# Shorter taps in a long depthwise convolution, and two weight units of a projection moved from one exact pass to three split passes

## The chip, the cores and the metric

The kernel runs on one core of a Trainium2 chip. The metric is device time in microseconds (us) of one execution. TensorE (PE in the profile) multiplies matrices, VectorE (DVE) and ScalarE (ACT) do elementwise work, GpSimd (POOL) a little of it, and SyncE (SP) issues the transfers from memory. Each engine works through its own queue in a fixed order; an instruction that waits holds up all that stand behind it in its queue.

## What is computed

Two transformer-like blocks on 256 tokens of 1024 channels, all in float32. The first block normalises the input, multiplies it by `w_in`, and sends the parts to a conformer branch and a state-space branch; their outputs are gated, added and multiplied by `w_o`, and a feed-forward part follows. The second block has two attentions and a mixture of 32 experts. The change lies in the first block:

```python
def causal_dwconv(x, w, b):          # x (B,T,C), w (K,C), b (C)
    k = w.shape[0]
    y = lax.conv_general_dilated(
        x, w[:, None, :].astype(x.dtype), window_strides=(1,),
        padding=[(k - 1, 0)], dimension_numbers=("NWC", "WIO", "NWC"),
        feature_group_count=x.shape[-1])
    return y + b.astype(x.dtype)

def conformer_branch(u_glu, dw_w, dw_b, ln_g, ln_b, w_out):
    a, g = jnp.split(u_glu, 2, axis=-1)
    v = a * jax.nn.sigmoid(g)
    v = causal_dwconv(v, dw_w, dw_b)                  # 31 taps, 1024 channels
    v = jax.nn.silu(layer_norm(v, ln_g, ln_b))
    return v @ w_out

def ssd_branch(...):
    ...
    return yn @ w_out                                 # w_ssm_out, 2048 x 1024

# in the block
mix = (sigmoid(gate_a) * y_a + sigmoid(gate_b) * y_b) @ w_o
```

Output token t of the long convolution is the bias plus the sum over s = 0 to 30 of weight 30 - s times input token t - s; for t - s below 0 there is nothing to add.

## The kernel before

Weights lie in memory as a stream of units of 128 x 2048 float32 (1 MB), read in turn into a ring of five buffers (`stream`, L213). A unit is multiplied in one of two ways (`passes`, L273). In **mode 4** the float32 unit goes straight to TensorE, which takes four times the array's time for it; the profile records each such matmul as two. In **mode 3** the unit is split in halves into a rounded part and a rest, `whl` (`split`, L260): ScalarE writes the rounded part (L261), VectorE the rest (L262), and TensorE then makes three quick matmuls for each one (`order`, L294: high by high, low by high, high by low). Mode 3 is the default; the table `MODES` (L1631) lists the units in mode 4. There are four `whl` buffers (`HL`, L31).

The work of the first block, in the order of the program: normalise; the gated input of the convolution (`glu`, four pairs of units, L597), written by VectorE into `vpad` behind 30 zero columns (L601, zeros at L592); the state-space branch in four groups (L686 to L778); the gates `ga` and `gb` (L793). Then `split_act` (L804) splits the state-space output `ynT` into `ynT_h` and `ynT_l`, and its product with `w_ssm_out` follows in eight units `ws0` to `ws7` of 128 output channels, two per call of `ssm_out` (L806); each call ends in one VectorE instruction on `gate_gb` (L809). `ssm_out(0)` stands ahead of the convolution's taps in the program, `ssm_out(1)` to `(3)` behind them (`WSJ`, L1630).

The convolution is VectorE's alone. `cacc` collects, for each of eight blocks of 128 channels, 31 taps (`tap`, L671): one TENSOR_SCALAR (L674) and 30 SCALAR_TENSOR_TENSOR (L676), each over 256 tokens; two blocks are worked in turn (L813). 8 times 31 are 248 instructions. When all are done, `pair_sums` (L818) adds the blocks in three steps `pair_cs`, TensorE sums over partitions (`cs`, L831), `cacc` is centred (L834), squared by ScalarE into the space of `vpad` (L836), summed again (`cq`, L842), and normalised into `cT`, which the units `wc` multiply (L864) after `ws7`.

The order on each engine is not written by hand. A scheduler takes the program, in which earlier lines come first among the instructions that are ready, plays it through with its own idea of durations, and fixes each engine's queue. So taps of early lines fill VectorE between the urgent instructions of the state-space branch, and every change of a size or of an instruction can move much of the queue.

```python
        for j in range(WSJ):
            ssm_out(j)
        for j in range(0, 8, 2):
            for k in range(CK):
                for i in (j, j + 1):
                    tap(i, k)
...
        for j in range(WSJ, 4):
            ssm_out(j)
```

Of the kernel before, what the change touches and what calls it, by code (L numbers as in the profile page):

```python
# [11 lines left out]
F32 = mybir.dt.float32  # L12
# [5 lines left out]
ALU = mybir.AluOpType  # L18
# [3 lines left out]
P = 128  # L22
T = 256
# [10 lines left out]
CK = 31  # L34
# [156 lines left out]
def block_kernel(ctx, tc, I, out, modes):  # L191
    nc = tc.nc
    V, S, G, PE = nc.vector, nc.scalar, nc.gpsimd, nc.tensor
# [19 lines left out]
    def stream(name):  # L213
        if name in ready:
            return ready[name][0], name
        off, kt, n = OFFSET[name]
        w = ring.tile([P, UNIT], F32, tag="w", name=f"w_{name}")
        src = I["stream"][off:off + P * kt * n].rearrange("(p m) -> p m", p=P)
        nc.sync.dma_start(w[:, :kt * n], src)
        return w[:, :kt * n].rearrange("p (k n) -> p k n", k=kt), name  # L220
# [12 lines left out]
    def par(name, i=0, n=1):  # L233
        second, o = PPO[name]
        return (pp2 if second else pp)[:, o + i:o + i + n]
# [33 lines left out]
    def act(pool, kt, name, tags=("ah", "al"), f=None):  # L269

        return Act(f, *(pool.tile([P, kt, T], F32R, tag=t, name=f"{name}_{t}") for t in tags))
# [40 lines left out]
    def gemm_chan(names, x, pool=mm, between={}):  # L312


        c, banks, put, last = 0, [], None, None
        for name in names:
            w, _ = stream(name)
            ps_ = passes(w, name)
            for i in range(w.shape[2] // P):
                if c % 2 == 0:  # L320
                    banks.append(bank(pool, f"ps_{name}_{i}").rearrange("p (c t) -> p c t", c=2))
                o = banks[-1][:, c % 2, :]
                if c in between:
                    with after(last):
                        put = between[c]()
                c += 1
                m = order(ps_, i * P, P)
                for j, (k, part, wp) in enumerate(m):
                    with after(put):
                        last = PE.matmul(o, wp, getattr(x, part)[:, k, :],  # L330
                                         start=(j == 0), stop=(j == len(m) - 1)).ins
        return banks
# [206 lines left out]
    with ExitStack() as e1:  # L539
        b1 = e1.enter_context(tc.tile_pool(name="b1", bufs=1, reuse_waits="tile"))  # L540
        hT = act(b1, 8, "hT")
        vpad = b1.tile([P, 8, T + CK - 1], F32, tag="vpad", name="vpad")
        cacc = b1.tile([P, 8, T], F32, tag="cacc", name="cacc")
        ynT = Act(b1.tile([P, 16, T], F32, tag="ynT", name="ynT"))
        gate = {n: b1.tile([P, 8, T], F32, name=f"gate_{n}") for n in ("ga", "gb")}
# [5 lines left out]
        with tc.tile_pool(name="pre", bufs=1, reuse_waits="tile") as pre:  # L551
# [15 lines left out]
            with tc.issue_after(hT.last), tc.issue_after(hT.act):  # L567
                ident_b = dcon.tile([P, P], BF16, name="ident_b")
                V.tensor_copy(ident_b, ident)
                ones = dcon.tile([P, P], F32, name="ones")  # L570
                V.memset(ones, 1.0)

                upper = dcon.tile([P, P], F32, name="upper")
                G.affine_select(out=upper, in_=ones, pattern=[[1, P]], compare_op=ALU.is_ge, fill=0.0, base=0, channel_multiplier=-1)
                strict = dcon.tile([P, P], F32, name="strict")
                G.affine_select(out=strict, in_=ones, pattern=[[-1, P]], compare_op=ALU.is_gt, fill=0.0, base=0, channel_multiplier=1)

                before_b = const.tile([P, P], BF16, name="before_b")
                V.tensor_tensor(before_b, upper, ident, op=ALU.subtract)

                pick = dcon.tile([P, 32], BF16, name="pick")
                V.tensor_tensor(pick, ident[:, 0:32], ident[:, 32:64], op=ALU.add)
                V.tensor_tensor(pick, pick, ident[:, 64:96], op=ALU.add)
                ones_b = const.tile([P, P], BF16, name="ones_b")
                V.memset(ones_b, 1.0)

                strict_b = dcon.tile([P, P], BF16, name="strict_b")
                V.tensor_scalar(strict_b, strict, NEG, None, op0=ALU.mult)
                slots = const.tile([P, CAP], F32, name="slots")
                G.iota(slots, pattern=[[1, CAP]], base=0, channel_multiplier=0, allow_small_or_imprecise_dtypes=True)  # L590
                iota8 = slots[:, :8]
                V.memset(vpad[:, :, :CK - 1], 0.0)  # L592
                S.activation(silu_c, par("c_2", 0, 8), AF.Silu)
                V.tensor_copy(cpad[:, :, 0], silu_c)


            for j in range(4):  # L597
                pa, pg = gemm_chan([f"glu{j}a0", f"glu{j}g0"], hT)
                sg = sg_pool.tile([P, 2, T], F32, tag="sg", name=f"sg{j}")
                S.activation(sg, pg, AF.Sigmoid)  # L600
                V.tensor_tensor(vpad[:, 2 * j:2 * j + 2, CK - 1:], pa, sg, op=ALU.mult)  # L601
                if j == 1:
                    nc.sync.dma_start(w_dt, I["w_dt"])
                    nc.sync.dma_start(rs, I["rs"].to_broadcast([P, NRS]))
                    nc.sync.dma_start(pp2, I["pp2"])
# [36 lines left out]
            for i in range(2):  # L642
                q = rs[:, RSO[f"lambda_q{i + 1}_2"]:RSO[f"lambda_q{i + 1}_2"] + 64]
                k = rs[:, RSO[f"lambda_k{i + 1}_2"]:RSO[f"lambda_k{i + 1}_2"] + 64]
# [24 lines left out]


        def tap(i, k):  # L671
            o = cacc[:, i, :]
            if k == 0:
                V.tensor_scalar(o, vpad[:, i, 0:T], par("conv_dw_w", i * CK), par("conv_dw_b", i), op0=ALU.mult, op1=ALU.add)  # L674
            else:
                V.scalar_tensor_tensor(o, vpad[:, i, k:k + T], par("conv_dw_w", i * CK + k), o, op0=ALU.mult, op1=ALU.add)  # L676


        def conv4(dst, ps_, c):
# [133 lines left out]
# [4 lines that stand above are left out]
# [12 lines left out]
        b = bank(sm, "cs")  # L829
        for i in range(2):  # L830
            PE.matmul(b[:, :T], ones, pair[:, i, :], start=(i == 0), stop=(i == 1))  # L831
        csq = vpad[:, :, :T]
        for i in range(0, 8, 2):
            V.scalar_tensor_tensor(cacc[:, i:i + 2, :], b[:, None, :T].to_broadcast(both), -1.0 / D, cacc[:, i:i + 2, :],  # L834
                                   op0=ALU.mult, op1=ALU.add)
# [21 lines left out]
        for n, i in ((4, "h"), (5, "l")):  # L857
            w = late.tile([P, 2, UNIT], F32, tag=f"ynT_{i}", name=f"w_ada{n}")
# [10 lines left out]
        for n in range(2):  # L869
            with tc.issue_after(cT.last):  # L870
                end = ada_v(n)
            for t, ps_ in enumerate(gemm_tok(f"wo{n}", mixT, 8, early=2 * n)):
                o = res[:, t, n * 512:(n + 1) * 512]
# [6 lines left out]
    with ExitStack() as e2:  # L880
# [17 lines left out]
        for j in range(11):  # L898
# [11 lines left out]
            for b, ps_ in enumerate(banks):  # L910
                o = b2.tile([P, 2, T], F32, tag=f"cv{b}", name=f"cv{b}_{j}", bufs=2)
                for i in range(2):
                    c = 22 * b + 2 * j + i
                    scale_bias(o[:, i, :], ps_[:, i, :], par("ffn_dw_w", 3 * c + 2), par("ffn_dw_b", c))
                    for s in range(1, 3):
                        V.scalar_tensor_tensor(o[:, i, s:], ps_[:, i, :T - s], par("ffn_dw_w", 3 * c + 2 - s), o[:, i, s:],
                                               op0=ALU.mult, op1=ALU.add)
# [5 lines left out]
        for n in range(2):  # L923
            end = ada_v(2 + n)
            for t, ps_ in enumerate(gemm_tok(f"dn{n}", guT, 22, early=2 * n)):
                o = res[:, t, n * 512:(n + 1) * 512]
# [22 lines left out]
    with ExitStack() as e3:  # L949
# [152 lines left out]
        for i in range(4):  # L1102
            (p1, r1), (p2, r2) = softmax_parts(qdT, kdT, i, "d")
            V.tensor_scalar(r2, r2, lam[:, 3:4], None, op0=ALU.mult)
            for q in range(2):
                V.tensor_scalar(p2[:, halves[q]], p2[:, halves[q]], r2[:, q:q + 1], None, op0=ALU.mult)
                V.scalar_tensor_tensor(p1[:, halves[q]], p1[:, halves[q]], r1[:, q:q + 1], p2[:, halves[q]],
                                       op0=ALU.mult, op1=ALU.add)
# [172 lines left out]
        for u in range(2):  # L1281
            w, nm = stream(f"wu1_{u}")
# [229 lines left out]
    for p in range(NE // 2):  # L1512
        last = p == NE // 2 - 1
        w = [fetched[12 * p + 2 * i:12 * p + 2 * i + 2] for i in range(6)]
# [113 lines left out]


WSJ = 1  # L1630
MODES = {n: 4 for n in ("ws0", "ws1", "ws2", "ws3", "wo1_1", "dn1_5", "qm_1", "glu0a0")}  # L1631


# [12 lines left out]
```

## Time and profile before

| what | before |
|---|---|
| median of three runs | 1231.01 us (1229.98 to 1234.34) |
| profiled execution | 1230.77 us, of which span 1229.1 us |
| PE busy | 1193.9 us (97%) |
| DVE busy | 778.5 us (63%) |
| ACT busy | 501.5 us (41%) |
| read from memory | 350.68 MB, 286 GB/s over the span |
| L676, the taps | 240 instructions, 100.7 us |

The span is the time from the first to the last instruction in the trace. Two records of one engine may overlap, so the time from start to start can be shorter than an instruction's own duration. The busy share of 63% on DVE is a mean over stages: up to about 300 us into the span it is nearly always busy, later far less. In the last 430 us the experts' weights are read at about 420 GB/s, the highest rate of the profile.

### The profile page before, as it was taken

The numbers are of one execution on the slowest core, as the hardware profiler recorded it, in microseconds if no ns is written. First come the engines' busy times: TensorE is split into PE (matmuls) and PEld (weight loads), VectorE is DVE, ScalarE is ACT, GpSimd is POOL, SyncE is SP. The second block draws the span as 40 slices with busy tenths as digits, with TensorE's granted clock in tenths as the row PEclk, the third lists the DMA queues.
The fourth block names the chain that finished last, engine by engine and source line by source line (L and its number), as shares of the span: only waits on it lengthen the run. The fifth ranks groups of instructions, "written<-read, shape, count | busy, mean of one in ns | idle before, by whom it ended". The sixth has DMA issues, their size and how long they took to land. (4 is left out here: it accounts for less than half of the span.)

```text
span 1229.1 us, 19383 instructions
## 1 busy us (share of the span) xinstructions
PE 1193.9 (97%) x7867; PEld 873.9 (71%) x7867; DVE 778.5 (63%) x1524; ACT 501.5 (41%) x831; POOL 27.5 (2%) x39
## 2 busy tenths in 40 slices
PE   7999999999999999999999999999999999999996
PEld 6989998898978999885888889544444444444443
DVE  6999999899877989667786676623322222332222
ACT  6456787743536666534345554411111111111111
POOL 0000100100000000001000000000000000000000
PEclk9999999999999999999999999999999999999999
DMA  9645343325777656764796347899999999999996
GB/s 361 237 144 198 113 171 104 138 103 206 292 269 296 240 194 219 283 211 167 298 383 268 116 144 294 330 412 421 423 419 423 420 424 420 423 420 423 422 420 244
DMA packets 51917, 353.03 MB, mean 287 GB/s; under 512 B 6000, under 2 KB 6640, under 8 KB 10224
## 3 DMA queue, kind: packets, MB, share of 16 engines
q1 hardware_dynamic: 51824, 351.75, 72.8%
q8 instruction: 63, 1.03, 0.3%
q14 instruction: 30, 0.25, 0.1%
HBM read 350.68 MB, written 1.05 MB: 286 GB/s over the span
## 5 line engine op out<-in xcount | busy, mean ns | idle before, releaser
L1534 DVE TENSOR_TENSOR hid<-hid,pu 128x256 f32<-128x256 f32 x32 | 12.0, 418 | 187.6 <-PE pu L1526 187.6
L1526 PE MATMUL pu<-we,xg 128*64 128x512 f32 x512 | 116.2, 593 | 4.6 <-DMA we<-in_experts 4.6
L1583 PE MATMUL pd<-we,hdT 128*64 128x512 f32 x512 | 113.4, 595 | 1.5 <-DVEq L1422 1.5
L1526 PE MATMUL pg<-we,xg 128*64 128x512 f32 x512 | 113.4, 592 | 0.0
L676 DVE SCALAR_TENSOR_TENSOR cacc<-vpad,pp,cacc 128x256 f32<-128x256 f32 x240 | 100.7, 477 | 0.0
L1526 PEld LDWEIGHTS pu<-we,xg 128*64 128x64 f32 x512 | 37.4, 137 | 80.5 <-issue 69.5
L1526 PEld LDWEIGHTS pg<-we,xg 128*64 128x64 f32 x512 | 37.8, 137 | 72.2 <-issue 69.8
L1583 PEld LDWEIGHTS pd<-we,hdT 128*64 128x64 f32 x512 | 35.9, 137 | 67.7 <-issue 64.9
L261 ACT ACTIVATE osb<-ob 128x512 fp32r<-128x512 f32 x31 | 19.5, 630 | 120.5 <-DVE ob L1587 120.5
L1546 ACT ACTIVATE hdT<-ht 128x512 f32<-128x512 f32 x16 | 9.6, 597 | 142.5 <-PE ht L1545 142.5
L1361 DVE TENSOR_SCALAR xg<-xg,s,mod 128x128 f32<-128x128 f32 x64 | 21.9, 404 | 65.9 <-PE xg L1337 63.7
L341 PE MATMUL ps_dn<-whl_dn,guT_gh 128*128 128x512 f32 x168 | 53.8, 398 | 0.0
L330 PE MATMUL ps_xs<-hT_ah,whl_xs 128*128 128x256 f32 x256 | 47.2, 282 | 0.0
L1587 DVE SCALAR_TENSOR_TENSOR ob<-pd,wpl,g 128x512 f32<-128x512 f32 x31 | 23.3, 751 | 37.4 <-PE pd L1583 34.8
L1529 ACT ACTIVATE hid<-pg 128x512 f32<-128x512 f32 x16 | 9.6, 597 | 82.5 <-PE pg L1526 82.4
L341 PE MATMUL ps_z<-whl_z,hT_ah 128*128 128x512 f32 x128 | 41.6, 398 | 0.1
L330 PEld LDWEIGHTS ps_xs<-hT_ah,whl_xs 128*128 128x128 f32 x256 | 39.6, 188 | 0.0
L341 PEld LDWEIGHTS ps_dn<-whl_dn,guT_gh 128*128 128x128 f32 x168 | 31.6, 188 | 7.7 <-issue 0.2
L495 DVE SCALAR_TENSOR_TENSOR sb_ada<-w_ada,silu_c,sb_ada 128x512 f32<-128x512 f32 x49 | 36.6, 747 | 0.6
L262 DVE TENSOR_TENSOR whl_dn<-w_dn,whl_dn 128x1024 fp32r<-128x1024 f32 x21 | 25.7, 1225 | 17.4 <-ACT whl_dn L261 17.3
L262 DVE TENSOR_TENSOR obl<-ob,osb 128x512 fp32r<-128x512 f32 x31 | 21.5, 693 | 21.6 <-ACT osb L261 21.6
L261 ACT ACTIVATE whl_dn<-w_dn 128x1024 fp32r<-128x1024 f32 x21 | 22.2, 1059 | 30.0 <-PE ps_dn L341 25.4
(760 smaller groups left out, 3111.8 us busy)
## 6 DMA issues: line engine op xcount, KB each, us to landing
we<-in_experts SPq DMA_DIRECT2D x189, 1024.0 KB, 19.8
w_ada<-in_stream SPq DMA_DIRECT2D x22, 1024.0 KB, 7.1
w_dn<-in_stream SPq DMA_DIRECT2D x10, 1024.0 KB, 4.8
w_xs<-in_stream SPq DMA_DIRECT2D x8, 1024.0 KB, 4.8
w_z<-in_stream SPq DMA_DIRECT2D x8, 1024.0 KB, 4.8
w_ws<-in_stream SPq DMA_DIRECT2D x8, 1024.0 KB, 4.8
w_bc<-in_stream SPq DMA_DIRECT2D x4, 1024.0 KB, 4.8
w_ga<-in_stream SPq DMA_DIRECT2D x4, 1024.0 KB, 4.8
```

What stands on the lines that cost most here:

```text
L261: a = S.activation(h, f, AF.Copy)
L262: return a.ins, V.tensor_tensor(l, f, h.bitcast(F32), op=ALU.subtract).ins
L330: last = PE.matmul(o, wp, getattr(x, part)[:, k, :], start=(j == 0), stop=(j == len(m) - 1)).ins
L341: PE.matmul(banks[t], getattr(x, p_)[:, u + k, t * P:(t + 1) * P], wp, start=(u == 0 and j == 0), stop=(u + kt == ktot and j == len(m) - 1))
L495: V.scalar_tensor_tensor(a, w[:, q, :], c, a, op0=ALU.mult, op1=ALU.add)
L676: V.scalar_tensor_tensor(o, vpad[:, i, k:k + T], par("conv_dw_w", i * CK + k), o, op0=ALU.mult, op1=ALU.add)
L1361: spreads.append(V.tensor_scalar(xg[:, k, :], src, s2[:, k:k + 1], mod[:, 24 + k:25 + k], op0=ALU.mult, op1=ALU.add).ins)
L1526: m = PE.matmul(pgu[i // 2][64 * e:64 * e + 64, :], xg[:, 4 * (i % 2) + k, 64 * e:64 * e + 64], w[i][e][:, k, :], start=(i % 2 == 0 and k ...
L1529: S.activation(hd, pgu[0], AF.Silu)
L1534: V.tensor_tensor(hd[:, c], hd[:, c], pgu[1][:, c], op=ALU.mult)
L1583: m = PE.matmul(pd[64 * e:64 * e + 64, :], hdT[:, f, 64 * e:64 * e + 64], w[4 + h][e][:, f, :], start=(f == 0), stop=(f == 3))
L1587: V.scalar_tensor_tensor(o[:, c], pd[:, c], wpl, g2[:, h, c], op0=ALU.mult, op1=ALU.mult)
```

## The change

The convolution's input has no zeros in front any more: `vpad` becomes `vg`, 256 columns wide, and the instruction that wrote the zeros is gone. A tap that reaches back s tokens adds input columns 0 to 255 - s to output columns s to 255, so it covers 256 - s columns. The taps run in the opposite order: the one with s = 0 comes first (it sets all columns and adds the bias), the one with s = 30 last. `csq`, the space for the squares, is now `vg` itself. And `ws2` and `ws3` leave the table `MODES`: they are split and multiplied in three passes as `ws4` to `ws7` were.

```diff
-        vpad = b1.tile([P, 8, T + CK - 1], F32, tag="vpad", name="vpad")
+        vg = b1.tile([P, 8, T], F32, tag="vg", name="vg")
...
-                V.memset(vpad[:, :, :CK - 1], 0.0)
...
-                V.tensor_tensor(vpad[:, 2 * j:2 * j + 2, CK - 1:], pa, sg, op=ALU.mult)
+                V.tensor_tensor(vg[:, 2 * j:2 * j + 2, :], pa, sg, op=ALU.mult)
...
         def tap(i, k):
-            o = cacc[:, i, :]
-            if k == 0:
-                V.tensor_scalar(o, vpad[:, i, 0:T], par("conv_dw_w", i * CK), par("conv_dw_b", i), op0=ALU.mult, op1=ALU.add)
+
+            k = CK - 1 - k
+            o, w = cacc[:, i, CK - 1 - k:], par("conv_dw_w", i * CK + k)
+            if k == CK - 1:
+                V.tensor_scalar(o, vg[:, i, :], w, par("conv_dw_b", i), op0=ALU.mult, op1=ALU.add)
             else:
-                V.scalar_tensor_tensor(o, vpad[:, i, k:k + T], par("conv_dw_w", i * CK + k), o, op0=ALU.mult, op1=ALU.add)
+                V.scalar_tensor_tensor(o, vg[:, i, :T - (CK - 1 - k)], w, o, op0=ALU.mult, op1=ALU.add)
...
-        csq = vpad[:, :, :T]
+        csq = vg
...
-MODES = {n: 4 for n in ("ws0", "ws1", "ws2", "ws3", "wo1_1", "dn1_5", "qm_1", "glu0a0")}
+MODES = {n: 4 for n in ("ws0", "ws1", "wo1_1", "dn1_5", "qm_1", "glu0a0")}
```

The scheduler then lays out the queues anew from about the second group of the state-space branch on. Two places matter. The first is VectorE's queue at the end of the taps (L676 before, L677 now), where `gate_gb` is the end of `ws0` and `ws1`, `pair_cs` the sums of all taps, and `whl_ws` the split of a half unit of `ws`. Before:

```order
L676 SCALAR_TENSOR_TENSOR cacc<-vpad,pp,cacc 128x256 x37
L809 SCALAR_TENSOR_TENSOR gate_gb<-gate_gb,ps_ws_0_2899 128x512
L676 SCALAR_TENSOR_TENSOR cacc<-vpad,pp,cacc 128x256 x23
L821 TENSOR_TENSOR pair_cs<-cacc 128x512
L262 TENSOR_TENSOR whl_ws_0_3275<-w_ws_3273,whl_ws_0_3275 128x1024
L823 TENSOR_TENSOR pair_cs<-pair_cs,cacc 128x512
```

With the change:

```order
L677 SCALAR_TENSOR_TENSOR cacc<-vg,pp,cacc 128x232 x2
L810 SCALAR_TENSOR_TENSOR gate_gb<-gate_gb,ps_ws_0_2898 128x512
L677 SCALAR_TENSOR_TENSOR cacc<-vg,pp,cacc 128x231 x2
L677 SCALAR_TENSOR_TENSOR cacc<-vg,pp,cacc 128x230 x2
L677 SCALAR_TENSOR_TENSOR cacc<-vg,pp,cacc 128x229 x2
L677 SCALAR_TENSOR_TENSOR cacc<-vg,pp,cacc 128x228 x2
L677 SCALAR_TENSOR_TENSOR cacc<-vg,pp,cacc 128x227 x2
L677 SCALAR_TENSOR_TENSOR cacc<-vg,pp,cacc 128x226 x2
L822 TENSOR_TENSOR pair_cs<-cacc 128x512
L262 TENSOR_TENSOR whl_ws_0_3236<-w_ws_3234,whl_ws_0_3236 128x1024
L824 TENSOR_TENSOR pair_cs<-pair_cs,cacc 128x512
```

The number of taps behind `gate_gb` falls from 23 to 12. The first split of `ws` stands behind the last tap and the first `pair_cs` in both, but before it belonged to `ws4` and now it belongs to `ws2`.

The second place is TensorE's queue from the first `ws` unit on (`w_ws` is a unit in mode 4, `whl_ws` a split half; `cs` is the sum over partitions that ends the taps). Before:

```order
L330 MATMUL ps_ws_0_2899<-ynT,w_ws_2897 128x256 x16
L330 MATMUL ps_ws_0_2899<-ynT,w_ws_2916 128x256 x16
L330 MATMUL ps_ws_0_3237<-ynT,w_ws_3235 128x256 x16
L330 MATMUL ps_ws_0_3237<-ynT,w_ws_3254 128x256 x16
L831 MATMUL cs<-pair_cs,ones 128x256 x2
L330 MATMUL ps_ws_0_3281<-ynT_h,whl_ws_0_3275 128x256
```

With the change:

```order
L330 MATMUL ps_ws_0_2898<-ynT,w_ws_2896 128x256 x16
L330 MATMUL ps_ws_0_2898<-ynT,w_ws_2915 128x256 x16
L330 MATMUL ps_ws_0_3242<-ynT_h,whl_ws_0_3236 128x256
L330 MATMUL ps_ws_0_3242<-ynT_l,whl_ws_0_3236 128x256
L330 MATMUL ps_ws_0_3242<-ynT_h,whl_ws_0_3236 128x256
```

Before, four units in mode 4 stood ahead of `cs`. Now two do, and right behind them come matmuls of `ws2` that read a split half; `cs` follows after 26 of those.

## Rows read from the trace of the kernel before

**Rows 1.** The page, busy time of TensorE, and its granted clock in 40 slices.

```profile
PE 1193.9 (97%) x7867; PEld 873.9 (71%) x7867; DVE 778.5 (63%) x1524; ACT 501.5 (41%) x831; POOL 27.5 (2%) x39
...
PEclk9999999999999999999999999999999999999999
```

**Rows 2.** Busy time by stretch: PE, PEld, DVE, ACT, POOL, clock, DMA share, GB/s.

```profile
265.00:280.00 15.00, 15.00 (x71) 13.22 (x70) 15.00 (x39) 2.54 (x3) 0.00 (x0) 1.00 0.26 75
280.00:295.00 15.00, 13.96 (x67) 12.01 (x66) 15.00 (x31) 0.00 (x0) 0.00 (x0) 1.00 0.41 146
```

**Rows 3.** Waits of PE, 264 to 420 us: total, times, longest; the longest one.

```profile
PE cs L831 <- DVE pair_cs L823: 1.0, 1, 1.0
```

**Rows 4.** Waits of PE, 20 to 265 us, all of them.

```profile
PE pcs L659 <- DVE a L656: 0.8, 1, 0.8
PE bt L724 <- DVE xd L716: 0.8, 2, 0.6
```

**Rows 5.** Timeline of PE from `ws0` to `wc`: start, length, instruction, [idle before].

```profile
264.74 27.79 PE L330 MATMUL ps_ws<-ynT,w_ws 128*128 128x256 f32 x128
293.57 1.13 PE L831 MATMUL cs<-pair_cs,ones 128*128 128x256 f32 x4 [1.04 <-DVE pair_cs L823]
294.35 0.47 PE L330 MATMUL ps_ws<-ynT_h,whl_ws 128*128 128x256 f32 x1
294.66 0.28 PE L330 MATMUL ps_ws<-ynT_l,whl_ws 128*128 128x256 f32 x1
...
295.13 0.28 PE L330 MATMUL ps_ws<-ynT_l,whl_ws 128*128 128x256 f32 x1
...
318.61 0.28 PE L330 MATMUL ps_wc<-cT_ah,whl_wc 128*128 128x256 f32 x1
```

**Rows 6.** Timeline of DVE at the end of the taps.

```profile
261.19 3.25 DVE L676 SCALAR_TENSOR_TENSOR cacc<-vpad,pp,cacc 128x256 f32<-128x256 f32 x8
...
265.01 14.73 DVE L676 SCALAR_TENSOR_TENSOR cacc<-vpad,pp,cacc 128x256 f32<-128x256 f32 x37
279.66 0.67 DVE L809 SCALAR_TENSOR_TENSOR gate_gb<-gate_gb,ps_ws 128x512 f32<-128x512 f32 x1
280.26 9.19 DVE L676 SCALAR_TENSOR_TENSOR cacc<-vpad,pp,cacc 128x256 f32<-128x256 f32 x23
289.37 0.68 DVE L821 TENSOR_TENSOR pair_cs<-cacc 128x512 f32<-128x512 f32 x1
289.97 1.21 DVE L262 TENSOR_TENSOR whl_ws<-w_ws,whl_ws 128x1024 fp32r<-128x1024 f32 x1
```

**Rows 7.** Groups of one form: busy us, mean ns of one, for other widths.

```profile
L676 DVE SCALAR_TENSOR_TENSOR cacc<-vpad,pp,cacc 128x256 f32<-128x256 f32 x240 | 100.7, 477 | 0.0
L495 DVE SCALAR_TENSOR_TENSOR sb_ada<-w_ada,silu_c,sb_ada 128x512 f32<-128x512 f32 x49 | 36.6, 747 | 0.6
...
L683 DVE SCALAR_TENSOR_TENSOR xsT<-ps_xs,pp,xsT 128x255 f32<-128x255 f32 x16 | 7.3, 479 | 0.9 <-ACT xsT L681 0.8
...
L683 DVE SCALAR_TENSOR_TENSOR xsT<-ps_xs,pp,xsT 128x253 f32<-128x253 f32 x16 | 7.0, 473 | 0.0
```

**Rows 8.** Timeline of PE: its first instructions, and the same transposes later.

```profile
9.04 1.97 PE L365 MATMUL tr_h<-ident,xn 128*128 128x128 f32 x8 [9.04 <-ACT xn L402]
...
20.52 0.47 PE L330 MATMUL ps_glu0g<-hT_ah,whl_glu0g 128*128 128x256 f32 x1
...
370.01 1.09 PE L365 MATMUL tr_h<-ident,xn 128*128 128x128 f32 x8
```

**Rows 9.** Busy time by stretch, columns as in rows 2: the end of the span.

```profile
1222.00:1225.00 3.00, 0.06 (x1) 0.00 (x0) 1.67 (x5) 1.80 (x5) 1.10 (x2) 1.00 0.07 25
1225.00:1229.00 4.00, 0.00 (x0) 0.00 (x0) 0.40 (x1) 0.37 (x1) 0.00 (x0) 0.71 0.66 243
```

**Rows 10.** The experts: one stretch, columns as in rows 2.

```profile
900.00:950.00 50.00, 49.48 (x304) 22.33 (x302) 14.43 (x40) 7.38 (x16) 0.00 (x0) 1.00 1.01 421
```

**Rows 11.** Waits of SP's queue, 600 to 1229 us: one before the experts.

```profile
SPq L534 <- DVE mgT_kd L1180: 14.9, 1, 14.9
```

## The prediction

> **What bounds the kernel now.** I read the page first: TensorE is busy 97% of the span, so its idle time is the thing to look for [rows 1]. That share is a mean over stages, so I went by stretch to where the change lies. From 265 to 295 us VectorE is busy without a pause and ScalarE, in the second half, does nothing; TensorE loses a little [rows 2]. The waits of TensorE say what that little is: one wait of 1.0 us for `pair_cs`, the end of the taps [rows 3]. Before 265 us all its waits together are 1.6 us [rows 4]. So two engines run level here: TensorE works off the units `ws`, VectorE the taps, and they meet at `cs`. The reader is to see in the two timelines [rows 5, 6] how the meeting is arranged. TensorE spends 27.79 us on `ws0` to `ws3` in mode 4, and none of that needs VectorE. In just that time VectorE does its last 60 taps and `pair_cs`. The four units are the cover of the taps.
>
> **Part 1, the taps get shorter.** The cost per column comes from one instruction at two widths: 477 ns at 256 columns, 747 ns at 512, so (747 - 477) / 256 = 1.05 ns a column [rows 7]. A tap reaching back s tokens loses s columns; 1 to 30 sum to 465, times 8 blocks is 3720 columns, times 1.05 ns is 3.9 us off VectorE. Tap starts at odd columns should cost nothing: the short convolution already writes 253 to 255 columns from column 1, 2 or 3 on, at 473 to 479 ns [rows 7]. The zero-fill of 30 columns is gone too; it lies in the first 30 us, where TensorE is fed by transfers and ScalarE, and I count it as nothing (if it were on the path it could give 0.3 us at most, as it is shorter than a tap of 477 ns). `vg` in place of `vpad`, and the squares written into it, are the same instructions.
>
> **Part 2, `ws2` and `ws3` in three passes.** A unit in mode 4 is 32 records; 128 records took 27.79 us [rows 5], so 6.95 us a unit. In mode 3 it is 48 matmuls, and four of them start 0.47 us apart from first to fifth [rows 5], 0.1175 us each, so 5.64 us. TensorE's own work falls by 2 x 1.31 = 2.6 us. VectorE gets four splits more of 1.21 us [rows 6], about 4.8 us, ScalarE four as well, while it is idle [rows 2]. On balance VectorE's work is about level (-3.9, +4.8).
>
> **Part 3, what the new order does with it.** This decides. The queues shown with the change have `ws2` right behind `ws1` on TensorE, and `ws2` needs its split, which stands on VectorE behind the last tap and the first `pair_cs`. TensorE has nothing else in between: it must stand still from the end of `ws1` until the taps are done. The queue behind the waiting matmul holds `cs`, `ws3` to `ws7`, and `wc`, all of the rest.
>
> - `ws1` ends at 264.74 + 64 x 0.217 = 278.6 us [rows 5].
> - The split of `ws2` ends, reckoned one way, by VectorE's work: taps end at 289.37 less 3.9 = 285.5, `pair_cs` takes 0.60, the split 1.21 [rows 6], so 287.3 us.
> - Reckoned another way, by the order: `gate_gb`, which ends `ws0` and `ws1`, ran at 279.66 [rows 6]. Twelve taps stand behind it with the change, 25 to 30 columns short, each (289.37 - 280.26) / 23 = 0.396 us less 0.029, so 4.4 us together. 279.66 + 0.60 + 4.4 + 0.60 + 1.21 = 286.5 us.
> - It can't be much earlier: `gate_gb` waits for `ws1` at 278.6, which gives 285.4 us.
>
> I take 286.9, midway between the two reckonings. TensorE stands idle for 8.3 us, where it stood 1.04 us.
>
> After that VectorE has the next half unit ready 1.2 to 2.4 us after the last (a `pair_cs` lies between the first ones), and TensorE needs 24 x 0.1175 = 2.8 us for one, so it runs without a pause. From the start of `ws4` to `wc` it took 318.61 - 294.35 = 24.26 us [rows 5]; now 96 matmuls more, 11.3 us, and `cs` (294.35 - 293.57 = 0.78 us) lie in the same stretch: 36.3 us. `wc` starts at 286.9 + 36.3 = 323.2 in place of 318.61, **4.6 us later**. This agrees with the parts: 7.3 us more idle time less 2.6 us of work. With the two reckonings and the earliest case the term is 3.1 to 5.0 us; as TensorE might lose less than its 1.6 us of waits ahead of this place [rows 4], I let it reach down to 1.5.
>
> **Part 4, TensorE's clock.** The trace of before has no idle time of this length between matmuls. It has two places that bound the price. Behind the 1.04 us at `cs` the clock stays at 1.00 [rows 2], price 0. At the start, after 9.04 us without work, eight transposes take 1.97 us where the same eight later take 1.09 [rows 8]: half speed, though the clock column reads 9 or more tenths from the first slice on [rows 1]. And at the end of the span the clock falls to 0.71 in the mean of the last 4 us, while TensorE has done 0.06 us in the 7 us up to there [rows 9], so part of the stretch is on the lower of the two levels, 1.2 GHz. The price of the start: from 9.04 to 20.52 us are 11.48 us for 16 transposes and the 32 records of `glu0a`; at the later pace 2 x 1.09 + 32 x 0.217 = 9.1. That is 2.4 us. An idle of 8.3 us is far nearer to 9.04 than to 1.04, so I take 2.0 us, ends 0 and 2.4.
>
> By the column of the clock alone, which shows no fall before the end, there would be no such term. The Trainium skill (TensorE: Matmul & The Clock Gate, Part 1) says otherwise and speaks against this change: half rate is the default of an idle array, and only activity lifts it. By the column the sum is 1235.4, by the rule 1237.4; the halved pace of the first transposes agrees with the rule.
>
> **The sum.** The profiled execution took 1230.77 us, 0.24 below the median of the runs. 1230.77 + 4.6 + 2.0 = **1237.4 us**. A shift at 318 us reaches the end because TensorE does without a pause what follows, and the experts' transfers, which run at their top rate later [rows 10], are not issued early of their own: their main burst waits for a result of the second block's attention, `mgT` [rows 11], and shifts with it.
>
> **Rivals.**
>
> *The clock holds* (0.14). The idle time comes as reckoned and costs nothing beyond. For it: the column of the clock. Against it: rows 8 and 9. Time 1235.4.
>
> *The experts swallow it* (0.08), no slower than before. In the last stage transfers fill the queues (DMA share 1.01) and TensorE is busy 49.48 of 50 us [rows 10]. If the weights arrived by a clock of their own, the delay would only eat into time that TensorE later spends waiting for them, and the end would stay: 1230.8. The point from which this holds: the burst of rows 11 would have to start at the same time in the run as now. Against it: it waits 14.9 us for VectorE's result, which is late by the same 6.6 us.
>
> *The taps don't get cheaper* (0.08). If short taps cost what long ones do, the taps end at 289.37 as before and the split at 291.2. TensorE is idle 12.6 us, `wc` starts 291.2 + 36.3 = 327.5, 8.9 later, and the clock takes its full 2.4: 1242.1. Against it: the two widths of rows 7.
>
> **How the numbers follow.** A measurement of this kernel can tell about 0.5% from no change, 6.2 us here, so from 1237.2 on it is slower. My forecast has 0.62, and with its terms of 1.5 to 5.0 and 0 to 2.4 it runs from about 1232.5 to 1238.2 and a little beyond for what the new order does elsewhere; its middle is just above the bound, so 0.34 of it is slower and 0.28 the same. The clock's rival (0.14) and the experts' (0.08) are the same, the taps' (0.08) slower. What I have not seen (0.08), such as another course of the state-space groups in the new order, I give 0.03, 0.03 and 0.02 to faster, same and slower. Sums: faster 0.03, same 0.53, slower 0.44. The range for 8 in 10 takes in my forecast, the clock's rival and the experts' case (0.84 together), 1230.0 to 1241.0; it leaves out the taps' case and most of the unseen.
>
> **What would show it.** Taps of L677 falling from 477 ns to about 446 at 226 columns. TensorE idle for 7 to 9 us just ahead of the first `whl_ws` matmul, put down to VectorE's `whl_ws`; `wc` 3 to 7 us later than 318.61; the first matmuls behind the gap at about 0.235 us from start to start in place of 0.1175, if the clock falls. No change of the stretch from `wc` to the end. I would be wrong if that gap is under 4 us (the order doesn't cost what I read from it), or if the end doesn't follow `wc`.

## The result, and the profile after

The changed kernel takes 1243.5 us (median of 6 runs, 1241.8 to 1247.5) where the kernel before took 1231.4 beside it: ratio 1.0106, 95% interval 1.0095 to 1.0116. It is slower by 1.1%, nearly twice what was forecast, and outside the range. The profiled execution took 1243.87 us with a span of 1242.1, 13.0 longer than before.

The page of the changed kernel, TensorE's busy time and granted clock, against [rows 1]:

```profile
PE 1195.1 (96%) x7899; PEld 874.4 (70%) x7899; DVE 779.7 (63%) x1527; ACT 503.9 (41%) x833; POOL 26.9 (2%) x39
...
PEclk9999999998999999999999999999999999999998
```

All engines do as much as before, within 3 us; the 13 us are time in which TensorE stands or works slowly. Setting the starts of the same matmuls side by side in the two traces shows where:

| stretch | lost there (us) | forecast |
|---|---|---|
| start to first `bc` matmul (63.03, now 61.65) | -1.4 | 0 |
| `bc` to `ws0` (264.74, now 266.30) | +2.9 | 0 |
| `ws0` to first `wc` (318.61, now 324.14) | +4.0 | +6.6 |
| `wc` to the last `qm` matmul (585.15, now 592.13) | +1.5 | 0 |
| from there to the last `pu` matmul (1207.29, now 1214.61) | +0.3 | 0 |
| last `pu` to the last `pd` matmul (1218.62, now 1231.70) | +5.8 | 0 |

`bc` is the first product of the state-space branch, `qm` one of the second block's attention; `pu` and `pd` are products of the experts, which are worked in 16 pairs, and `pd` of the last pair is TensorE's last large piece of work.

The stretch that I had reckoned with gives less than forecast, and more than half of the loss lies at places that I had put at nothing. Four stretches of the changed kernel (busy PE, PEld, DVE, ACT, POOL, clock, DMA share, GB/s) show the clock behind three of these places:

```profile
89.00:91.00 2.00, 1.51 (x6) 1.21 (x7) 1.74 (x5) 1.95 (x4) 0.00 (x0) 0.87 0.00 0
91.00:93.00 2.00, 2.00 (x6) 1.62 (x5) 1.99 (x8) 1.99 (x3) 0.00 (x0) 0.50 0.04 8
...
280.00:295.00 15.00, 8.96 (x57) 8.34 (x56) 15.00 (x28) 2.31 (x4) 0.00 (x0) 0.77 0.46 158
...
1223.00:1227.00 4.00, 3.66 (x10) 1.36 (x12) 0.00 (x0) 0.00 (x0) 0.00 (x0) 0.50 0.09 32
```

The third, 280 to 295 us, stands against the second row of [rows 2]: 8.96 us of work where there were 13.96, at 0.77 of the clock where it was 1.00. A clock of 0.50 is the lower level, 1.2 GHz, through the whole stretch.

**Place one, near 89 us.** TensorE's timeline, the `z` matmuls of the first state-space group:

```profile
86.31 0.61 PE L786 MATMUL pdec<-a__111,upper 128*128 128x32 f32 x4
89.49 0.50 PE L341 MATMUL ps_z<-whl_z,hT_ah 128*128 128x512 f32 x1 [2.57 <-ACT zs L704]
```

It waits for `zs`, an activation. ScalarE's timeline there, changed kernel:

```profile
82.19 1.01 ACT L682 ACTIVATE xsT<-ps_xs,pp 128x256 f32<-128x256 f32 x2
86.51 0.56 ACT L682 ACTIVATE bcT<-ps_bc,pp 128x256 f32<-128x256 f32 x1 [3.31 <-DVE bcT L684]
86.98 0.56 ACT L682 ACTIVATE xsT<-ps_xs,pp 128x256 f32<-128x256 f32 x1
87.55 1.28 ACT L704 ACT_TABLE_LOAD   x1
88.84 0.60 ACT L704 ACTIVATE zs<-ps_z 128x512 f32<-128x512 f32 x1
```

and of the kernel before:

```profile
83.40 1.01 ACT L681 ACTIVATE xsT<-ps_xs,pp 128x256 f32<-128x256 f32 x2
84.43 1.28 ACT L703 ACT_TABLE_LOAD   x1
87.58 0.60 ACT L703 ACTIVATE zs<-ps_z 128x512 f32<-128x512 f32 x1 [1.87 <-PE ps_z L341]
88.84 0.57 ACT L681 ACTIVATE bcT<-ps_bc,pp 128x256 f32<-128x256 f32 x1 [0.66 <-DVE bcT L683]
```

Before, the table was loaded and `zs` ran the moment `ps_z` was there. Now `bcT` and `xsT` stand ahead of it, ScalarE waits 3.31 us for VectorE's `bcT`, and only then loads the table. Nothing in this code was edited: the scheduler, with the taps changed, chose another order.

**Place two, `ws2`.** TensorE and VectorE of the changed kernel, against [rows 5] and [rows 6]:

```profile
279.92 0.47 PE L330 MATMUL ps_ws<-ynT_h,whl_ws 128*128 128x256 f32 x1
...
281.87 0.27 PE L330 MATMUL ps_ws<-ynT_l,whl_ws 128*128 128x256 f32 x1
288.19 2.29 PE L330 MATMUL ps_ws<-ynT_h,whl_ws 128*128 128x256 f32 x9 [6.04 <-DVE whl_ws L262]
...
290.53 1.78 PE L832 MATMUL cs<-pair_cs,ones 128*128 128x256 f32 x4
291.96 0.47 PE L330 MATMUL ps_ws<-ynT_h,whl_ws 128*128 128x256 f32 x1
```

```profile
281.30 0.69 DVE L810 SCALAR_TENSOR_TENSOR gate_gb<-gate_gb,ps_ws 128x512 f32<-128x512 f32 x1
281.90 4.50 DVE L677 SCALAR_TENSOR_TENSOR cacc<-vg,pp,cacc 128x231 f32<-128x231 f32 x12
286.30 0.69 DVE L822 TENSOR_TENSOR pair_cs<-cacc 128x512 f32<-128x512 f32 x1
286.90 1.23 DVE L262 TENSOR_TENSOR whl_ws<-w_ws,whl_ws 128x1024 fp32r<-128x1024 f32 x1
```

The wait is the one forecast, for the split behind the last tap. But it stands inside `ws2`: 16 matmuls (high by high and low by high, from 279.92 on) need only ScalarE's rounded half and run ahead of it; the last 8, high by low, need VectorE's rest. From the end of `ws1` to the split, 279.92 to 288.19, it is 8.27 us; 2.2 of them were filled.

**Place three, the last `pd` group.** The changed kernel, then the kernel before:

```profile
1217.53 0.38 PE L1563 MATMUL cm<-ident,ow 128*128 128x128 f32 x2
1223.34 8.95 PE L1584 MATMUL pd<-we,hdT 128*64 128x512 f32 x32 [5.43 <-DMA we<-in_experts]
```

```profile
1210.21 0.38 PE L1562 MATMUL cm<-ident,ow 128*128 128x128 f32 x2
1212.12 7.09 PE L1583 MATMUL pd<-we,hdT 128*64 128x512 f32 x32 [1.53 <-DVEq L1422]
```

A wait of 5.43 us where 1.53 stood, and 8.95 us for the group where it took 7.09: 3.9 and 1.9 us, the 5.8 of the table. The profile names the weights in one and the branch in the other (L1422, now L1423: in `past_capacity`, the one branch in the kernel, which jumps over code that this input does not need). The labels contradict each other, so this place needed experiments.

### The profile page after: what moved, and what is told of

Read it like the earlier page. It is cut to its first block, busy times and chain, and to the rows that moved or that the text cites. A ratio compares the mean times of both kernels' runs of the same rounds, so it can differ in the third digit from the quotient of the medians.

```text
span 1242.1 us, 19456 instructions
## 1 busy us (share of the span) xinstructions
PE 1195.1 (96%) x7899; PEld 874.4 (70%) x7899; DVE 779.7 (63%) x1527; ACT 503.9 (41%) x833; POOL 26.9 (2%) x39
## 5 line engine op out<-in xcount | busy, mean ns | idle before, releaser
L677 DVE SCALAR_TENSOR_TENSOR cacc<-vg,pp,cacc 128x255 f32<-128x255 f32 (+14 forms) x240 | 97.4, 463 | 0.1
L330 PE MATMUL ps_ws<-ynT_h,whl_ws 128*128 128x256 f32 x192 | 35.7, 289 | 6.0 <-DVE whl_ws L262 6.0
```

The lines of the kernel that those rows point to most:

```text
L330: last = PE.matmul(o, wp, getattr(x, part)[:, k, :], start=(j == 0), stop=(j == len(m) - 1)).ins
L677: V.scalar_tensor_tensor(o, vg[:, i, :T - (CK - 1 - k)], w, o, op0=ALU.mult, op1=ALU.add)
```

## Experiments

**e1 and e2: the two halves apart.** e1 is the changed kernel with the old table, e2 the kernel before with the new one.

```diff
-MODES = {n: 4 for n in ("ws0", "ws1", "wo1_1", "dn1_5", "qm_1", "glu0a0")}
+MODES = {n: 4 for n in ("ws0", "ws1", "ws2", "ws3", "wo1_1", "dn1_5", "qm_1", "glu0a0")}
```

> The shortened taps alone; all four units of the state-space output product run in four passes as in the kernel before. Theory: the 12 us are four separate losses, and two of them (6.0 us of idle TensorE ahead of the last 8 matmuls of ws2, and the 5.4 us ahead of the last pd group at the end, which comes from the length of TensorE's own program) go with the passes, while the 2.6 us wait for the zs activation near 86 us goes with the taps, since ScalarE's order there is that of the changed kernel. Then: a wait of about 2.6 us for zs, none at ws2, cs not waiting for pair_cs, and about 1.5 us at the last pd as before; 1232 us (1230 to 1234). Rival A, all of the loss follows from the ws2 wait and taps only help: 1228 us or less (3.9 us of taps less the clock). Rival B, the late pd group is a matter of late weights whatever the program: 5 us more at the end, 1237 to 1238 us.

> The padded full-length taps of the kernel before; only ws2 and ws3 in three passes. Theory: no wait for zs; TensorE runs ws0, ws1 and 16 matmuls of ws2 until about 280.5 us and then stands until the split behind the last tap and the first pair sum ends near 291.2 us, 10 to 11 us; minus 1.0 of the old wait and 2.6 of saved passes, plus about 3 us of half clock: the first wc matmul near 328 us (10 later than before), and 5.4 us at the last pd as in the changed kernel, since TensorE's program has its length: 1246 us (1243 to 1250). Rival A (the ws2 wait is all that the passes cost): 1241 us. Rival B (late weights at the end whatever the program): either.

e1: 1234.52 us, ratio 1.0026 (1.0015 to 1.0038). e2: 1246.79 us, 1.0131 (1.0117 to 1.0146). The longest waits of TensorE, 20 to 420 us, in e1:

```profile
PE ps_z L341 <- ACT zs L704: 2.6, 1, 2.6
PE pcs L658 <- DVE a L655: 1.0, 1, 1.0
PE cs L832 <- DVE pair_cs L824: 0.8, 1, 0.8
```

and in e2:

```profile
PE ps_ws L330 <- DVE whl_ws L262: 10.6, 1, 10.6
```

Each wait follows its half: `zs` the taps, `ws2` and the late `pd` (1.53 us in e1, 5.51 in e2) the passes. Rival A falls in both: the taps alone are slower and not faster, and e2 lies 5.8 us above its 1241. In e1 `cs` still waited 0.8 us, which I had not expected, and the clock fell once more, near 780 us; it came out 2.5 us above my number and just above its range. The halves don't add up (3.7 and 15.9 make 19.6, the whole lost 12.1). Most of that lies at `ws2`, where the changed taps cut the wait from 10.6 to 6.0 us: from `ws0` to `wc` e1 loses 0.4 us, e2 10.2 and the changed kernel 4.0, so 6.6 of the 7.5 us.

**e3 and e4: a longer program for TensorE.** Each kernel with 64 idle matmuls in the expert stage:

```diff
-                m = PE.transpose(b[:, t * P:(t + 1) * P], owf[:, t, :], ident).ins
+                m = PE.transpose(b[:, t * P:(t + 1) * P], owf[:, t, :], ident).ins; [PE.matmul(b[:, 511:512], ident, ident[:, :1], start=True, stop=True) for _ in range(2)]
```

> The kernel before with 64 one-column matmuls added to the expert stage, four in each of the 16 pairs, behind the cm transposes, where TensorE waits for weights from time to time; nothing reads what they write. TensorE's program before the last branch is then as many matmuls longer as that of the changed kernel (64). Theory (the late pd group comes from where the branch's target falls in TensorE's program): the wait ahead of the last pd group grows from 1.5 to about 5.4 us, part of the group runs at half clock, and the time is 1237 us (1235 to 1239). Rival B (late weights): the wait stays near 1.5 us, time 1231 to 1233 us.

> The changed kernel with the same 64 one-column matmuls in the expert stage. Theory: the branch's target moves on by another 64 matmuls with their weight loads; the wait ahead of the last pd group falls from 5.4 to about 1.5 us, with no half clock there, and the time is 1238 us (1236 to 1240). Rival B (late weights, since the stage began 7 us later): 5 us stay, 1243 to 1245 us.

e3: 1235.61 us, 1.0034 (1.0021 to 1.0047), the wait 1.52 us. e4: 1247.74 us, 1.0128 (1.0112 to 1.0145), the wait 4.47 us. Both kept the wait that they had, as rival B has it, and the theory as I had put it falls. (Both take some 4 us more than without the pad, and more than rival B had. The added matmuls are busy 16.1 us in each trace, the waits of `pu` for weights, 4.6 and 5.3 us without the pad, are gone, and near 780 us both have a stretch at half clock.) But the counts showed that this was no test of it. The queue that fetches TensorE's instructions, changed kernel and e4:

```profile
q8 instruction: 63, 1.03, 0.3%
```

```profile
q8 instruction: 64, 1.05, 0.3%
```

One fetch of 16 KB more, and 128 matmuls with their 128 weight loads more in the trace: I had added 256 instructions, just one such page, so that everything behind kept its place in its page. The changed kernel has 32 matmuls and 32 loads more than the one before, 64 instructions.

**e6 and e7: the same with other counts.** The same line with `ident[:1, :1]` in 1 x 1 matmuls, three for each pair of experts in e6 (changed kernel, 48) and one in e7 (kernel before, 16).

> The changed kernel with 48 matmuls of 1 x 1 in the expert stage, three in each pair. In e3 and e4 each added matmul showed as two matmuls and two weight loads in the trace, 256 instructions in all, and one instruction fetch of 16 KB more (64 for 63): a whole page, which left the branch's target where it was in its page. 48 make 192 instructions; with the 64 that the changed kernel has more than the one before that is a whole page again. Theory (the target's place in its page decides): the wait ahead of the last pd group 1.5 us, no half clock there; 1238 us (1236 to 1240). Rival (late weights): about 5 us as in e4, 1243 to 1248 us.

> The kernel before with 16 matmuls of 1 x 1 in the expert stage, one in each pair: 64 instructions, as many as the changed kernel has more. Theory (the branch target's place in its page): the wait ahead of the last pd group grows from 1.5 to about 5 us, 3 to 7 us of half clock follow; 1236 us (1234 to 1239). Rival (late weights): 1.5 us, 1231 to 1232 us.

e6: 1238.6 us, 1.0063 (1.0049 to 1.0077). e7: 1236.63 us, 1.0047 (1.0033 to 1.0061). TensorE's timeline of e6, then of e7:

```profile
1219.97 7.09 PE L1584 MATMUL pd<-we,hdT 128*64 128x512 f32 x32 [1.52 <-DVEq L1423]
```

```profile
1218.24 9.78 PE L1583 MATMUL pd<-we,hdT 128*64 128x512 f32 x32 [5.84 <-PEq L1422]
```

Both turned over. The kernel before, with 16 matmuls whose result nothing reads, gets the late `pd` group; the changed kernel, with 48, loses it. Late weights are excluded: e6 has the same transfers and does not wait. Over all kernels the wait goes by the number of TensorE instructions ahead of the branch, counted from the kernel before and less whole pages of 256:

| more instructions | kernels | wait at the last `pd` (us) |
|---|---|---|
| 0 | before, e1, e3, e5, e6, e11 | 1.5 |
| 32 | e8 | 1.5 |
| 64 | changed, e2, e4, e7, e9 | 4.5 to 5.8 |
| 168 | e10 | 1.5 |

In e8 the group itself takes 8.01 us at full clock, where the others without the wait take 7.09; why was not tried. That it is the branch, and not something else at this place, rests on where it stands in the program and on the fetches told of at the end; a kernel without it was not run.

**e5: `zs` put first.** e1, with the second halves of the `conv4` work of the first group issued behind the first `zs`:

```diff
-                for t, ps_ in enumerate(gemm_tok(f"z{g}", hT, 8)):
-                    S.activation(zs[:, t, :], ps_, AF.Silu)
...
+                    pz = gemm_tok(f"z{g}", hT, 8)
+                    z0 = S.activation(zs[:, 0, :], pz[0], AF.Silu).ins
+                    with after(z0 if g == 0 else None):
...
+                    S.activation(zs[:, 1, :], pz[1], AF.Silu)
```

> The shortened taps alone (e1) with one thing more: in the first state-space group the second halves of the conv4 work are put behind the activation zs of the first 128 tokens, so that ScalarE's order there is that of the kernel before. Theory (the taps' loss in e1 is the 2.6 us wait for zs and the half clock behind it, because the new tap lengths gave ScalarE another order): no wait for zs, no half clock near 90 us; the first wc matmul 4.3 us earlier than in e1, near 317 us; 1230 us (1228.5 to 1232.5, the upper end if the clock falls once near 575 or 780 us as in e1 and e3). Rival (the groups run at VectorE's pace, and a wait removed here comes back as another): 1234 to 1235 us as e1, with the lost time as TensorE idle elsewhere between 90 and 265 us.

1230.03 us, ratio 0.9998 (0.9989 to 1.0008), 4.5 us less than e1. No wait for `zs`; the longest of TensorE from 20 to 420 us is now

```profile
PE pcs L658 <- DVE a L655: 1.0, 1, 1.0
```

The first `wc` is at 317.3 us, 4.2 before that of e1, where 4.3 was expected. But 0.9 of it lies ahead of the first `bc` matmul (61.9 in e5, 62.8 in e1), where it is no gain of this edit. From `bc` to `wc` it takes 255.4 us, in e1 258.7, in the kernel before 255.6: the order cost 3.3 us. So the taps' loss ahead of `wc` in e1 was ScalarE's order. What in the taps' edit tips the scheduler (the lengths, their opposite order, the zero-fill that is gone) was not tried apart. In this run the clock fell near 570 us as in the changed kernel. The changed kernel, e5 and, at full clock, the kernel before:

```profile
578.00:582.00 4.00, 3.77 (x10) 2.75 (x10) 3.91 (x11) 3.97 (x8) 0.00 (x0) 0.57 0.97 349
```

```profile
571.50:575.50 4.00, 3.77 (x10) 2.78 (x10) 3.92 (x11) 3.97 (x8) 0.00 (x0) 0.58 0.96 360
```

```profile
573.00:577.00 4.00, 3.77 (x15) 2.74 (x15) 3.91 (x11) 3.97 (x8) 0.00 (x0) 1.00 0.99 368
```

Same work, same gaps (3.77 of 4.00 us in all three), two clocks. e3, whose program up to there is that of the kernel before, has the fall as well; e1, e6 and e8 don't. So the 1.5 us of this stretch are not the change's.

**e8 and e9: `ws2` split early.** e8 is e5 with `ws2` in three passes (`ws3` in four) and its split ahead of the taps; e9 the changed kernel with that line alone.

```diff
+        prepare("ws2")
         for j in range(0, 8, 2):
             for k in range(CK):
```

> e5 with ws2 in three passes, ws3 in four, and ws2's weights split ahead of the taps in the program, so that the split does not stand behind the last tap. Theory: no wait ahead of the last matmuls of ws2; ws2 takes 5.6 us and not 6.95, the taps end 2.4 us later, which ws3 covers: the first wc matmul 1.3 us earlier than in e5. TensorE's program is 32 instructions longer than before, and the wait at the last pd group 1.5 us or about 5, by where the target falls: 1229 us (1227 to 1231) or 1234 us. Rival (VectorE's two splits of 1.2 us push cs, and with it wc, back by what TensorE saves): wc as in e5.

> The changed kernel with ws2's weights split ahead of the taps in the program. Theory (what TensorE waits for is the split's place behind the taps): no wait inside ws2; the wait moves to ws3, whose own split still stands behind the last tap and the first pair sum, now 2.4 us later (near 290.5 us), while TensorE has the rest of ws2 and the first 16 matmuls of ws3 to do until about 288 us: 2 to 3 us of idle time where 6.0 stood, and half of the half clock behind it at most; the first wc matmul 3 to 5 us after that of the changed kernel less its shift, near 320 us; 1239 us (1237 to 1241). Rival (VectorE's total is what counts, wherever the splits stand): first wc matmul near 324 us as in the changed kernel, 1243 us.

e8: 1229.24 us, 0.9993 (0.9984 to 1.0002). `wc` starts at 315.9, 1.4 before e5, where 1.3 was expected; counted from `ws0` it is 52.2 us against 54.1 in e5, 1.9 less. The saved pass arrives whole, with 0.6 us more whose cause stays open. e9: 1239.47 us, 1.0077 (1.0063 to 1.0090), no wait inside `ws2`, and in all of 264 to 420 us these two for the units `ws`, for the next split and for ScalarE's half, where 2 to 3 us were expected:

```profile
PE ps_ws L330 <- DVE whl_ws L262: 1.0, 1, 1.0
PE ps_ws L330 <- ACT whl_ws L261: 0.6, 1, 0.6
```

From `ws0` to `wc` it takes 52.6 us, where the changed kernel took 57.8 and the kernel before 53.9. So not VectorE's total but the split's place made the loss.

**e10: TensorE kept at work through the wait.**

```diff
+                    if name == "ws2" and i == 0 and j == 16:
+                        with after(last):
+                            keep_warm(26, ss, "ws2")
```

> The changed kernel with 26 matmuls of 128 x 128 on the identity, into a bank that nothing reads, between the first 16 matmuls of ws2 and the 8 that wait for the split, so that TensorE works through the wait. Theory (the idle time costs itself and then a stretch at half clock, which showed as 6.8 us): no half clock between 280 and 295 us, the wait for the split still ends near 288 us, and the first wc matmul comes 3.4 us earlier, near 321 us; 1240 us if the wait at the last pd group stays at 5 us, 1235 us if the 104 instructions more bring it to 1.5. Rival (the clock is not to be held by such work, or the matmuls of the half clock were waiting for VectorE's next splits in any case): first wc matmul at 324 us.

1236.53 us, 1.0049 (1.0035 to 1.0062). That is 7.0 us below the changed kernel, but 5.8 of them are the last `pd` group, which waits 1.53 us here and runs at full clock. The stretch from 280 to 295 us, and TensorE's timeline at `ws2`:

```profile
280.00:295.00 15.00, 14.33 (x112) 13.63 (x112) 14.91 (x31) 2.20 (x3) 0.00 (x0) 1.00 0.37 131
```

```profile
283.43 5.97 PE L303 MATMUL warm_ws<-ident 128*128 128x128 f32 x52
289.63 1.32 PE L333 MATMUL ps_ws<-ynT_h,whl_ws 128*128 128x256 f32 x9 [0.23 <-DVE whl_ws L262]
...
291.97 1.13 PE L835 MATMUL cs<-pair_cs,ones 128*128 128x256 f32 x4 [0.43 <-DVE pair_cs L827]
292.75 0.47 PE L333 MATMUL ps_ws<-ynT_h,whl_ws 128*128 128x256 f32 x1
```

The clock holds at 1.00, and the 8 matmuls behind the split with the one after them take 1.32 us and not 2.29. But from the split to the first matmul behind `cs` it takes 292.75 - 289.63 = 3.12 us, in the changed kernel 291.96 - 288.19 = 3.77: 0.65 us saved, not 3.4. The first `wc` matmul starts at 324.5, where the theory had 321 and the rival 324; counted from `ws0` it is 56.8 us against 57.8, 1.0 less. TensorE now waits 0.43 us for `pair_cs`; at half pace it had merely been slow where VectorE was slow too. The rival's second form holds for most of it.

**e11: all three together** (the changed kernel with the edits of e5, e9 and e6).

> The changed kernel with three things put right together: the zs order of e5, ws2's split ahead of the taps as in e9, the 48 matmuls of e6. Theory (these three places hold all of the loss): no wait for zs; 2 to 3 us of idle time at ws3; 1.5 us at the last pd group; 1232 us (1230 to 1235). Rival (a part of the 12 us is still unnamed): above 1236 us.

1229.56 us, 0.9995 (0.9986 to 1.0004). It is below the 1230 to 1235 expected; the wait at the next split was 1.2 us and not 2 to 3. With the three places mended the 12 us are gone, so the rival falls. It is not shown that each other stretch is as before: from `bc` to `wc` e11 takes 253.4 us, 2.2 less than the kernel before, and from `wc` to `qm` 267.8, 1.3 more, without a fall of the clock; e9, with the same early split of `ws2`, has 1.1 more there, and in both the first `ps_ada` matmuls stand 13 us earlier in TensorE's order. This was not tried apart. e8 and e11 are the fastest kernels tried, but neither can be told from the kernel before.

## Why the prediction was wrong

- **Part 1 was right.** The group of the taps, against the first line of [rows 7]: 463 ns in the mean where it was 477, 97.4 us busy where it was 100.7, so 3.3 us of the 3.9 forecast; and 12 taps behind `gate_gb` in 286.30 - 281.90 = 4.40 us, the 4.4 forecast.

```profile
L677 DVE SCALAR_TENSOR_TENSOR cacc<-vg,pp,cacc 128x255 f32<-128x255 f32 (+14 forms) x240 | 97.4, 463 | 0.1
```

- **Part 3 had the mechanism and missed a detail.** "TensorE has nothing else in between: it must stand still from the end of `ws1`" is the step that failed: two of a unit's three passes don't need VectorE's half, so 16 matmuls, 2.2 us, filled the gap. It was 6.0 us, not 8.3, though the split came 8.27 us after the end of `ws1`, as reckoned. The 36.3 us from the split to `wc` counted these 16 once more. The order rows show those matmuls behind `ws1`; I did not ask which half each reads.
- **Part 4 foresaw the half clock**: it was 0.50 behind an idle time of 6.04 us. The Trainium skill (TensorE: Matmul & The Clock Gate, Part 1) says that half rate is the default and that activity lifts it; this stretch agrees. The size was off: 2.0 us taken, 0.65 to 1.0 by e10. I priced it from the start of the kernel; here TensorE at full clock waits 0.43 us for VectorE's `pair_cs`, so that part of what the clock gives back is lost again. Gap and clock together were forecast at +6.6 from `ws0` to `wc` and came to +4.0.
- **"I let it reach down to 1.5" was the failed step before 265 us.** I read this stretch only for what could be gained from its 1.6 us of waits [rows 4]. e1 and e5 show that the changed taps turned `zs` and `bcT` round on ScalarE, for 3.3 us from `bc` to `wc` by e5, 2.9 from `bc` to `ws0` in the changed kernel. The order of ScalarE could have been compared beforehand, as TensorE's was; "another course of the state-space groups" was named as unseen, with 0.08, and never priced.
- **"A shift at 318 us reaches the end because TensorE does without a pause what follows"** held until the last `pu` (+7.3 us there). Then the branch cost 5.8 us more, the largest single loss; less these 5.8 us the time lies in the range. "No change of the stretch from `wc` to the end" is the step that failed here: the wait at the branch was put at nothing, and the 64 instructions more that TensorE's program got raised it from 1.53 to 5.43 us and brought 1.9 us of half clock behind it. The sign named beforehand, that the end does not follow `wc`, came true: `wc` is 5.5 us later, the end 13.0. Without the branch the time would have been near 1238.6, as in e6, close to the forecast of 1237.4, but by luck: the `zs` wait left out and the gap and clock too large had nearly cancelled, and so did two terms that are not the change's, 1.4 us gained at the start and 1.5 lost at `qm`.
- **The rivals.** The experts swallowed nothing: the shift came through whole. The taps did get cheaper. The clock did not hold, though it cost little.

## What to carry to other kernels

Where a scheduler fixes the queues, compare the order on every engine over the whole stretch before the edit as well as behind it; the taps' change lost its time 190 us earlier than the place it was about. Before pricing a wait at the first instruction of a unit, ask which operand each pass reads. And where a program has a branch that is taken late, a few instructions more or less can cost as much as the change: lay pads of idle instructions of several lengths into both kernels before believing a difference of half a per cent; the pad of 256 here moved nothing, those of 64 and 192 did.

## What the runs showed of the hardware

At the kernel's one branch TensorE stood 1.5 us or 4.5 to 5.8 us, by the number of its instructions ahead of it. Its instructions came in fetches of 16 KB, 63 in the span; 256 instructions more made it 64. In the changed kernel one such fetch lies between 1220.3 and 1221.5 us, inside the wait; in the kernel before there is none in the wait, and one between 1212.1 and 1216 us, when `pd` has begun at 1212.12. The queue in these two stretches:

```profile
q8 instruction: 1, 0.02, 5.3%
```

```profile
q8 instruction: 1, 0.02, 1.5%
```

In e6 too there is none in the wait, in e7 one. The Trainium skill (Runtime: NRT & Kernel Launch, Instruction fetch mechanics) says that a taken branch whose target is not in the window already fetched forces a fetch before the engine goes on. The table of waits and these fetches agree with it. Where the window ends was not tried: only the shifts 0, 32, 64 and 168 were run.

The clock fell in some kernels' traces and not in others behind the same two idle times of 0.7 and 0.6 us near 570 us, and it was worth 1.5 us at `qm`. The slow pace at the start also ended earlier or later: in e3 the second eight transposes, near 11.9 us, took 1.26 us, in e7 1.92, and the first `bc` matmul came at 61.4 and 63.3 us, though both are the kernel before up to the experts. So the 1.4 us gained at the start in the table above are not the change's either.
